# The relative-bias table of a two-layer decoder trunk: bucket runs copied on GpSimd in place of one-hot products on TensorE

## The chip, the cores and the metric

The kernel runs on one core of a Trainium2 chip. A core has TensorE (matrix products, written to PSUM), VectorE and ScalarE (which read PSUM and SBUF), GpSimd (SBUF only) and the queues that issue DMAs: SP's, ScalarE's and GpSimd's. In the profile they are called PE (with PEld for the loading of its weights), DVE, ACT, POOL and SP. Each engine works through its own instructions in order, and engines wait for each other through semaphores. The metric is the device time of one launch in microseconds (us), the median over the runs.

## The reference: what is computed

One sequence of 512 tokens with 1024 channels in float32 goes through two layers. Layer 0 is a Mamba-2 mixer and a convolutional feed-forward block. Layer 1 is differential attention (8 heads, two softmax maps for each) with shared keys and values, and a second feed-forward block. The part that matters here is the bias that is added to the attention logits:

```
n = max(dist, 0)                       # dist = query position - key position
bucket = n                 if n < 16
         16 + floor(log(n / 16) / log(8) * 16), at most 31   otherwise
bias[h] = rel_bias[bucket, h]          # rel_bias: 32 buckets x 8 heads
logits = q . k * scale + bias          # where dist < 0: -inf
```

The bias depends on the distance alone. A row of 512 distances for each head is therefore all that has to be known. Buckets 0 to 15 hold one distance each. From bucket 16 on, a bucket is a run of neighbouring distances, and the last one, 31, holds all distances from 113 up.

## The kernel before: how the work is ordered

All large products are made on TensorE from float32 values that are split in a high and a low part, so that one product is three passes (`mm3`, L196 to L198; in the attention's projections L932 to L934). The weights come in chunks of 512 KB on SP's queue (`wr_...`, three buffers). ScalarE makes the high part of each chunk (`wh_...`, L165 where a gain is folded in), VectorE the low part (`wl_...`, L166), and TensorE then reads both. Chunks are fetched two ahead of their use.

Between the feed-forward block of layer 0 and the attention of layer 1 lies the stage that the change touches. The order of TensorE's work there is written out by hand (`tc.manual_schedule` for PE) and the other engines are ordered by a planner:

- `ps_d`: the last products of the down-projection (L196 to L198). With them the sum of squares of the stream is collected in `nacc_kv` (L498, mostly on GpSimd).
- `ps_k` for the first half of the heads: `proj("k0")`, four token blocks in four PSUM banks, weights `wh_k`/`wl_k`. After the first chunk, `norm_kv.col()` turns `nacc_kv` (L445 on TensorE) and computes the factor of the RMS norm from it on VectorE in a chain of small steps (`tr_nkv`, L447 and L420 to L428). The evacuation of each `ps_k` bank multiplies by this factor (`knk`, ScalarE L954). Sums of squares (L955, L956), the norm of the heads (L434 to L439, L963) and transposes on TensorE (`ktk`, L970) follow.
- `ps_q` for the first half of the heads in the same four PSUM banks, with weights `wh_q`/`wl_q`.

The table is made at the start of this stage. `rb` holds `rel_bias` as it stands in memory (32 buckets on 32 partitions, 8 heads along the row). The array `onehot`, made on the host, has a row for each bucket and a column for each of 640 places (127 places for negative distances, then 513 for the distances from 0). Its two halves `oh` of 320 columns each are loaded, TensorE multiplies them by `rb` (`ps_rb`, L914), ScalarE copies the results to `bv` (L915), VectorE sets the negative distances to -1e30 (L917), and SP's queue writes both halves to a scratch table `bd` in memory (L918). For each head, a DMA on SP's queue (`tr`, L1000) reads the table shifted by one place on each of 128 partitions, and VectorE copies it in reversed order to `tb` (L1001), which the logits read at L1020. `tr` has one buffer, so the DMA of the next head waits for the copy of the one before.

SP's queue holds the weights of the following chunks and the DMAs of the table one behind the other; what is queued behind a DMA that waits, waits too.

Of the kernel before, what the change touches and what calls it, by code (L numbers as in the profile page):

```python
# [9 lines left out]
F32 = mybir.dt.float32  # L10
F32R = mybir.dt.float32r
I32 = mybir.dt.int32
AF = mybir.ActivationFunctionType
# [5 lines left out]
P = 128  # L19
# [12 lines left out]
AH = 8  # L32
EPS = 1e-6
NEG = -1.0e30
LAM_INIT = 0.8 - 0.6 * math.exp(-0.3 * 1)
NBIAS = 640
# [3 lines left out]
def trunk_kernel(ctx: ExitStack, tc, x, ssm_ln_g, ssm_in_w, ssm_conv_w, ssm_conv_b, ssm_dt_bias,  # L40
                 ssm_a_log, ssm_d, ssm_norm_g, ssm_out_w, kv_ln_g, kv_w, k_norm_g, rel_bias,
                 attn_ln_g, q_w, q_norm_g, lam_vecs, subln_g, attn_out_w, ffn_ln_g, ffn_up_w,
                 ffn_conv_w, ffn_conv_b, ffn_down_w, onehot, out):
    nc = tc.nc
    act, dve, pool, pe, sync = nc.scalar, nc.vector, nc.gpsimd, nc.tensor, nc.sync

# [13 lines left out]
    def aux_bank(name):  # L60
        return pp.tile([P, T], F32, tag="aux", name=name)
# [176 lines left out]
    with tc.tile_pool(name="ph0", bufs=1) as p0:  # L238
# [24 lines left out]
        ps = aux_bank("pst")  # L263
# [91 lines left out]
        for l in range(2):  # L355
            for j in range(2):
                cols = slice(j * FFN, (j + 1) * FFN)
                d = sf[:, 2 * l + j, :]
# [22 lines left out]
        ps = aux_bank("pst")  # L381
# [134 lines left out]
    with tc.tile_pool(name="ssm_y", bufs=1) as yp, tc.tile_pool(name="ssm", bufs=1) as sp:  # L516
# [29 lines left out]
        ps = aux_bank("ps_dtt")  # L546
# [32 lines left out]
        ps = aux_bank("ps_dec")  # L579
# [15 lines left out]
        ps = aux_bank("ps_cum")  # L595
# [304 lines left out]
    with tc.tile_pool(name="att_o", bufs=1) as op_, tc.tile_pool(name="att", bufs=1) as ap:  # L900
# [1 line left out]
        late = []  # L902


        rb = ap.tile([32, AH], F32, name="rb")
        bd = dp.tile([AH, NBIAS], F32, name="bd")
        sync.dma_start(rb, rel_bias)
        hb = NBIAS // 2
        for i in range(2):
            oh = ap.tile([32, hb], F32, tag="p0", name="oh%d" % i, bufs=3)  # L910
            bv = ap.tile([AH, hb], F32, tag="p1", name="bv%d" % i, bufs=3)
            sync.dma_start(oh, onehot[:, i * hb:(i + 1) * hb])
            ps = aux_bank("ps_rb%d" % i)
            pe.matmul(ps[:AH, :hb], rb, oh, start=True, stop=True)  # L914
            act.activation(bv, ps[:AH, :hb], AF.Copy)  # L915
            if i == 0:
                dve.memset(bv[:, 0:P - 1], NEG)  # L917
            sync.dma_start(bd[:, i * hb:(i + 1) * hb], bv)  # L918

        kT = [ap.tile([P, 4, T], F32, name="kT%d" % i) for i in range(2)]  # L920
        qT = [ap.tile([P, 4, T], F32, name="qT%d" % i) for i in range(2)]
# [249 lines left out]
    ffn(1, norm1, bp, None, None)  # L1171


def _onehot():
    dist = np.maximum(np.arange(NBIAS) - (P - 1), 0)
    nf = np.maximum(dist, 1).astype(np.float32)
    large = 16 + (np.log(nf / np.float32(16)) / np.float32(math.log(8)) * np.float32(16)).astype(np.int32)
    bucket = np.where(dist < 16, dist, np.minimum(large, 31))
    return np.ascontiguousarray((np.arange(32)[:, None] == bucket[None, :]).astype(np.float32))


_INS = ['x', 'ssm_ln_g', 'ssm_in_w', 'ssm_conv_w', 'ssm_conv_b', 'ssm_dt_bias', 'ssm_a_log', 'ssm_d',
# [25 lines left out]
```

## Time and profile before

| | before |
|---|---|
| time, median of 3 runs (lowest to highest) | 1356.53 us (1356.06 to 1356.53) |
| span of the profiled execution | 1355.4 us |
| median less span: what lies around the span | 1.1 us |
| TensorE busy | 1347.2 us (99%) |
| VectorE busy | 911.1 us (67%) |
| ScalarE busy | 654.0 us (48%) |
| GpSimd busy | 95.7 us (7%) |
| granted TensorE clock, mean | 0.999 |

The span runs from the first to the last instruction of one profiled execution. The busy time of an engine counts its compute instructions, not its waits. Rows of the timeline give the start, the duration, the engine, the line of the kernel, the operation, what it writes and reads and the shapes; in square brackets stands the time that the engine was idle before, and what ended this. SPq and POOLq are the queues that issue DMAs; their rows show the issue, not the transfer. Matrix products overlap, so their spacing from start to start is the better measure.

### The profile page before, as it was taken

To read this page: it belongs to the slowest core of one execution; us is meant where nothing else is said; L and a number is where in the kernel's file an instruction comes from. 1 tells how busy PE (TensorE), PEld (TensorE's weight loads), DVE (VectorE), ACT (ScalarE), POOL (GpSimd) and SP (SyncE) were. 2 spreads that over 40 slices of the span, in tenths; PEclk is the share of its full clock that TensorE was granted. 3 is DMA by queue.
4 is the path that set the end of the run, shared out by engine and by line. 5 is a ranking of instruction groups with operands and counts; after the bars stand their busy time and mean duration, and the time that the engine had idled before them with its cause. 6 is when DMAs were issued, how large, how long until landed. Compare 5 with 4: busy or idle time off the path is not lost.

```text
span 1355.4 us, 16857 instructions
## 1 busy us (share of the span) xinstructions
PE 1347.2 (99%) x6421; PEld 1096.1 (81%) x6421; DVE 911.1 (67%) x1525; ACT 654.0 (48%) x1066; POOL 95.7 (7%) x120
## 2 busy tenths in 40 slices
PE   9999999999999999999999999999999999999998
PEld 7877887887888888888888777777888888888887
DVE  4989878688777774267754555778777773367742
ACT  5696844642444442234433556767654442134420
POOL 6230301200020000000001000000110000000000
PEclk9999999999999999999999999999999999999999
DMA  7462432432333333333323422221223333333322
GB/s 203 138 170 78 149 109 94 148 94 69 95 94 93 94 96 105 94 94 94 101 78 108 127 80 86 78 75 37 78 87 89 104 94 94 93 104 99 94 94 78
DMA packets 179905, 135.06 MB, mean 100 GB/s; under 512 B 6509, under 2 KB 163633, under 8 KB 179825
## 3 DMA queue, kind: packets, MB, share of 16 engines
q1 hardware_dynamic: 174048, 120.84, 30.2%
q0 software_dynamic: 4496, 12.05, 2.9%
q8 instruction: 50, 0.82, 0.3%
q10 hardware_dynamic: 1280, 1.10, 0.2%
q14 instruction: 31, 0.25, 0.1%
HBM read 131.72 MB, written 2.25 MB: 99 GB/s over the span
## 4 chain that ended last, share of the span: by engine, by line
PE 94%; DVE 2%; ACT 1%; DMA 1%; issue 1%; POOL 0%; SPq 0%; DVEq 0%; POOLq 0%; ACTq 0%
PE ps_g L197 6%; PE ps_g L196 6%; PE ps_g L198 6%; PE ps_u L197 6%; PE ps_u L196 6%; PE ps_u L198 6%; PE ps_in L198 5%; PE ps_in L197 5%; PE ps_in L196 5%; PE ps_d L851 3%; PE ps_d L197 3%; PE ps_d L196 3%; PE ps_d L853 3%; PE ps_d L852 3%; PE ps_d L198 3%; PE ps_o L198 2%
## 5 line engine op out<-in xcount | busy, mean ns | idle before, releaser
L196 PE MATMUL ps_u<-xgh,wh_u 128*128 128x512 f32 x352 | 137.4, 390 | 0.0
L197 PE MATMUL ps_g<-xgl,wh_g 128*128 128x512 f32 x352 | 137.0, 389 | 0.0
L196 PE MATMUL ps_g<-xgh,wh_g 128*128 128x512 f32 x352 | 137.0, 389 | 0.0
L198 PE MATMUL ps_u<-xgh,wl_u 128*128 128x512 f32 x352 | 137.0, 389 | 0.0
L198 PE MATMUL ps_g<-xgh,wl_g 128*128 128x512 f32 x352 | 137.0, 389 | 0.0
L197 PE MATMUL ps_u<-xgl,wh_u 128*128 128x512 f32 x352 | 136.9, 389 | 0.0
L196 PE MATMUL ps_in<-xgh,wh_in 128*128 128x512 f32 x304 | 120.9, 398 | 0.0
L197 PE MATMUL ps_in<-xgl,wh_in 128*128 128x512 f32 x304 | 120.8, 397 | 0.0
L198 PE MATMUL ps_in<-xgh,wl_in 128*128 128x512 f32 x304 | 119.6, 393 | 0.0
L151 DVE TENSOR_TENSOR wl_d<-wr_d,wh_d 128x1024 fp32r<-128x1024 f32 (+1 forms) x46 | 54.2, 1178 | 96.9 <-ACT wh_d L147 96.7
L147 ACT ACTIVATE wh_d<-wr_d 128x1024 fp32r<-128x1024 f32 (+1 forms) x46 | 47.1, 1024 | 130.6 <-PE ps_d L853 62.4
L875 ACT ACTIVATE hh<-vg 128x512 fp32r<-128x512 f32 x44 | 27.8, 632 | 114.9 <-DVE vg L874 114.9
L823 DVE TENSOR_TENSOR uu<-ps_u,nr_f 128x512 f32<-128x512 f32 x44 | 30.4, 692 | 78.0 <-PE ps_u L198 77.8
L198 PEld LDWEIGHTS ps_g<-xgh,wl_g 128*128 128x128 f32 x352 | 66.1, 188 | 13.8
L197 PEld LDWEIGHTS ps_g<-xgl,wh_g 128*128 128x128 f32 x352 | 66.0, 187 | 13.9 <-DVE xgl L413 0.3
L197 PEld LDWEIGHTS ps_u<-xgl,wh_u 128*128 128x128 f32 x352 | 66.2, 188 | 13.5
L196 PEld LDWEIGHTS ps_g<-xgh,wh_g 128*128 128x128 f32 x352 | 66.1, 188 | 13.6
L196 PEld LDWEIGHTS ps_u<-xgh,wh_u 128*128 128x128 f32 x352 | 66.1, 188 | 13.7
L198 PEld LDWEIGHTS ps_u<-xgh,wl_u 128*128 128x128 f32 x352 | 66.0, 188 | 13.7
L147 ACT ACTIVATE wh_g<-wr_g 128x1024 fp32r<-128x1024 f32 x44 | 46.7, 1062 | 51.6 <-PE ps_u L197 32.2
L196 PE MATMUL ps_d<-hh,wh_d 128*128 128x512 f32 x176 | 68.5, 389 | 0.0
L197 PE MATMUL ps_d<-hl,wh_d 128*128 128x512 f32 x176 | 68.5, 389 | 0.0
(348 smaller groups left out, 3176.7 us busy)
## 6 DMA issues: line engine op xcount, KB each, us to landing
wr_g<-in_ffn_up_w_dram SPq DMA_DIRECT2D x44, 512.0 KB, 3.8
wr_u<-in_ffn_up_w_dram SPq DMA_DIRECT2D x44, 512.0 KB, 3.9
wr_d<-in_ffn_down_w_dram SPq DMA_DIRECT2D x42, 512.0 KB, 3.6
wr_in<-in_ssm_in_w_dram SPq DMA_DIRECT2D x40, 512.0 KB, 3.9
m<-cumd POOLq DMA_DIRECT2D x16, 512.0 KB, 4.0
wr_out<-in_ssm_out_w_dram SPq DMA_DIRECT2D x16, 512.0 KB, 3.5
wr_k<-in_kv_w_dram SPq DMA_DIRECT2D x8, 512.0 KB, 3.8
wr_q<-in_q_w_dram SPq DMA_DIRECT2D x8, 512.0 KB, 3.8
```

What stands on the lines that cost most here:

```text
L147: return act.activation(self.wh[:, :self.n], self.raw[:, :self.n], AF.Copy)
L151: return eng.tensor_tensor(out=self.wl[:, :self.n], in0=self.raw[:, :self.n], in1=self.wh[:, :self.n].bitcast(F32), op=ALU.subtract)
L196: pe.matmul(ps, wh, xh, start=start, stop=False)
L197: pe.matmul(ps, wh, xl, start=False, stop=False)
L198: return pe.matmul(ps, wl, xh, start=False, stop=stop).ins
L823: dve.tensor_tensor(out=u, in0=ps, in1=r, op=ALU.mult)
L851: pe.matmul(pss[b], hh[k][:, ts], wh[:, k - k0, :], start=k == 0, stop=False)
L852: pe.matmul(pss[b], hh[k][:, ts], wl[:, k - k0, :], start=False, stop=False)
L853: pe.matmul(pss[b], hl[k][:, ts], wh[:, k - k0, :], start=False, stop=k == n - 1)
L875: act.activation(h, ga, AF.Copy)
```

## The change

The one-hot array and both products go. `rb` becomes 8 partitions (heads) by 32 (buckets): a DMA on GpSimd's queue reads `rel_bias` transposed, each of the 256 values from its own place in memory. GpSimd then writes both halves `bv` itself: one memset for the 127 negative distances, one copy of 16 columns for the buckets 0 to 15, and one copy for each bucket from 16 to 31, in which a column of `rb` is repeated over the run. Bucket 31 crosses the middle at column 320 and takes two copies (80 and 320 columns). That makes 18 copies. The two halves go to `bd` by DMAs on GpSimd's queue too. From `tr` on, all is as before.

```diff
-        rb = ap.tile([32, AH], F32, name="rb")
+        rb = ap.tile([AH, 32], F32, name="rb")
         bd = dp.tile([AH, NBIAS], F32, name="bd")
-        sync.dma_start(rb, rel_bias)
+        pool.dma_start(rb, rel_bias.rearrange("b h -> h b"))
         hb = NBIAS // 2
         for i in range(2):
-            oh = ap.tile([32, hb], F32, tag="p0", name="oh%d" % i, bufs=3)
             bv = ap.tile([AH, hb], F32, tag="p1", name="bv%d" % i, bufs=3)
-            sync.dma_start(oh, onehot[:, i * hb:(i + 1) * hb])
-            ps = aux_bank("ps_rb%d" % i)
-            pe.matmul(ps[:AH, :hb], rb, oh, start=True, stop=True)
-            act.activation(bv, ps[:AH, :hb], AF.Copy)
             if i == 0:
-                dve.memset(bv[:, 0:P - 1], NEG)
-            sync.dma_start(bd[:, i * hb:(i + 1) * hb], bv)
+                pool.memset(bv[:, 0:P - 1], NEG)
+            for b, a, e in _ranges():
+                a, e = max(a - i * hb, 0), min(e - i * hb, hb)
+                if a < e:
+                    src = rb[:, 0:e - a] if b == 0 else rb[:, b:b + 1].to_broadcast([AH, e - a])
+                    pool.tensor_copy(bv[:, a:e], src)
+            pool.dma_start(bd[:, i * hb:(i + 1) * hb], bv)
...
+def _ranges():
+    dist = np.arange(NBIAS - (P - 1))
...
+    at = P - 1 + np.searchsorted(bucket, np.arange(33))
+    return [(0, P - 1, int(at[16]))] + [(b, int(at[b]), int(at[b + 1])) for b in range(16, 32)]
```

In the program that results, TensorE's order is the same but for the two products, and ScalarE's but for the two copies. On SP's queue the five DMAs of `rb`, `oh` and `bd` are gone. On GpSimd the DMA of `rb` and the memset stand ahead of the last addition to `nacc_kv` (L498), and the 18 copies and the two DMAs behind it. On VectorE the planner puts the first copy to `tb` (L1001) into the chain of `tr_nkv`: before, it stood behind the chain's last step; now it stands behind L423, with nine steps of the chain (three times L426, L427, L428) still to come.

More of the change, by code (lines that the diff above doesn't have):

```diff
@@ L42, in trunk_kernel @@
                  attn_ln_g, q_w, q_norm_g, lam_vecs, subln_g, attn_out_w, ffn_ln_g, ffn_up_w,
-                 ffn_conv_w, ffn_conv_b, ffn_down_w, onehot, out):
+                 ffn_conv_w, ffn_conv_b, ffn_down_w, out):
     nc = tc.nc
@@ L1171, in trunk_kernel @@
     ffn(1, norm1, bp, None, None)
-def _onehot():
-    dist = np.maximum(np.arange(NBIAS) - (P - 1), 0)
+def _ranges():
+    dist = np.arange(NBIAS - (P - 1))
     nf = np.maximum(dist, 1).astype(np.float32)
@@ L1178, in _onehot @@
     bucket = np.where(dist < 16, dist, np.minimum(large, 31))
-    return np.ascontiguousarray((np.arange(32)[:, None] == bucket[None, :]).astype(np.float32))
+    at = P - 1 + np.searchsorted(bucket, np.arange(33))
+    return [(0, P - 1, int(at[16]))] + [(b, int(at[b]), int(at[b + 1])) for b in range(16, 32)]
 _INS = ['x', 'ssm_ln_g', 'ssm_in_w', 'ssm_conv_w', 'ssm_conv_b', 'ssm_dt_bias', 'ssm_a_log', 'ssm_d',
@@ L1201 @@
         add("in_%s_dram" % name, np.ascontiguousarray(inputs[name]))
-    add("onehot_dram", _onehot())
     args.append(nc.dram_tensor("out_0_dram", (1, T, D), F32, kind="ExternalOutput").ap())
```

## The prediction

> **What bounds the kernel now.** I read first the page (busy time and the chain of waits), then the timeline of all engines around the removed products, then VectorE, SP's queue and GpSimd alone in that stage, last those who use what this stage makes. The page:
>
> ```profile
> span 1355.4 us, 16857 instructions
> ...
> PE 1347.2 (99%) x6421; PEld 1096.1 (81%) x6421; DVE 911.1 (67%) x1525; ACT 654.0 (48%) x1066; POOL 95.7 (7%) x120
> ...
> PE 94%; DVE 2%; ACT 1%; DMA 1%; issue 1%; POOL 0%; SPq 0%; DVEq 0%; POOLq 0%; ACTq 0%
> ```
>
> TensorE is busy nearly throughout and carries 94% of the chain. A stretch taken out of its stream shortens the time by its length, unless something else now makes TensorE wait; an edit elsewhere costs nothing until TensorE waits for it. GpSimd is nearly idle.
>
> **What goes from TensorE.** The timeline where the two products stand:
>
> ```profile
> 746.71 0.39 PE L933 MATMUL ps_k<-wl_k,xgh 128*128 128x512 f32 x1
> ...
> 747.17 0.39 PE L932 MATMUL ps_k<-wh_k,xgh 128*128 128x512 f32 x1
> ...
> 747.67 0.12 PEld L914 LDWEIGHTS ps_rb<-oh,rb 32*8 32x8 f32 x2 [0.54 <-PE ps_k L932]
> 747.71 1.23 PE L914 MATMUL ps_rb<-oh,rb 32*8 32x320 f32 x4
> 747.98 0.08 PEld L914 LDWEIGHTS ps_rb<-oh,rb 32*8 32x8 f32 x1 [0.18 <-DMA oh<-onehot_dram]
> ...
> 748.87 0.50 PE L933 MATMUL ps_k<-wl_k,xgh 128*128 128x512 f32 x1
> ...
> 749.20 0.39 PE L934 MATMUL ps_k<-wh_k,xgl 128*128 128x512 f32 x1
> ```
>
> Two steps of the stream take 747.17 - 746.71 = 0.46 us, so 0.23 each. From 747.17 to 749.20 there are again two steps, but 2.03 us: the products run as four instructions, with the change of weights around them and a short wait for `oh`. All of it goes: 2.03 - 0.46 = 1.57 us saved on the path. ScalarE's two copies, VectorE's memset and five DMAs of SP's queue go too; none stood in TensorE's way, so I count nothing for them.
>
> **What is added: when does the table arrive?** Call X the time, on the clock of this profile, at which VectorE can start the first copy to `tb`. SP's queue and VectorE before:
>
> ```profile
> 743.27 0.37 SPq L139 DMA_DIRECT2D wr_q<-in_q_w_dram  x1
> 744.00 0.35 SPq L907 DMA_DIRECT2D rb<-in_rel_bias_dram  x1
> ...
> 752.91 0.35 SPq L1000 DMA_DIRECT2D tr<-bd  x1
> 753.56 0.40 SPq L139 DMA_DIRECT2D wr_q<-in_q_w_dram  x1
> ```
> ```profile
> L918 SPq DMA_DIRECT2D bd<-bv x2: 271/342/412, 749.3 to 749.8; - x2
> ```
> ```profile
> 753.86 0.16 DVE L426 TENSOR_TENSOR rst_nkv<-tr_nkv 128x4 f32<-128x4 f32 x1
> ...
> 755.43 0.17 DVE L428 SCALAR_TENSOR_TENSOR tr_nkv<-rst_nkv,tr_nkv 128x4 f32<-128x4 f32 x1
> 756.29 0.43 DVE L1001 COPY tb<-tr 128x512 f32<-128x512 f32 x1 [0.69 <-DMA tr<-bd]
> 757.73 1.42 DVE L166 SCALAR_TENSOR_TENSOR wl_q<-wr_q,c,wh_q 128x512 fp32r<-128x512 f32 x2 [1.02 <-ACT wh_q L165]
> ...
> 772.53 2.50 DVE L963 TENSOR_TENSOR knk<-knk,ssk 128x512 f32<-128x512 f32 x4
> ```
>
> X was 756.29. GpSimd's rows, its small DMAs, and the only table in this kernel that GpSimd's queue writes to memory and reads back (`cumd`):
>
> ```profile
> 0.31 0.10 POOL L1193 MEMSET const-float32-0.0<- 128x1 f32 x1 [0.31 <-issue]
> 0.35 0.10 POOL L1193 MEMSET const-float32-1.0<- 128x1 f32 x1
> ...
> 1.15 0.29 POOL L204 TENSOR_SCALAR_AFFINE_SELECT ident<-ones 128x128 f32<-128x128 f32 x1 [0.63 <-DVE ones L202]
> ...
> 7.27 0.18 POOL L249 COPY xgo<-xt 128x1 f32<-128x1 f32 x1 [5.34 <-DMA xt<-in_x_dram]
> 7.40 0.71 POOL L250 DMA_DIRECT2D st<-in_ssm_conv_b_dram  x1
> ...
> 53.65 0.57 POOL L601 DMA_DIRECT2D cumd<-cumT  x1 [21.64 <-ACT c L236]
> ...
> 56.08 1.07 POOL L622 DMA_DIRECT2D m<-cumd  x2 [1.13 <-DMA cumd<-cumT]
> ```
> ```profile
> L632 POOL TENSOR_SCALAR_AFFINE_SELECT m<-m x16: 1085/1091/2010, 60.3 to 247.6; 128x1024 f32<-128x1024 f32 x16
> ```
> ```profile
> 745.65 1.42 POOL L498 TENSOR_TENSOR nacc_kv<-nacc_kv,nsq_kv 128x512 f32<-128x512 f32 x1 [10.55 <-ACT nsq_kv L496]
> ```
> ```profile
> cumd<-cumT POOLq DMA_DIRECT2D x2, 64.0 KB, 1.8
> ...
> alog<-in_ssm_a_log_dram POOLq DMA_DIRECT2D x1, 16.0 KB, 4.6
> ...
> s2t<-in_ssm_d_dram POOLq DMA_DIRECT2D x1, 0.1 KB, 5.5
> ...
> s2t<-in_subln_g_dram POOLq DMA_DIRECT2D x1, 0.5 KB, 2.9
> ```
>
> Step by step:
> - *Load of `rb`.* Before, SP was free at 743.64 and issued at 744.00, so the place of the tile comes free then. GpSimd, idle since before 745.65, issues at 744.0 too. It then has the memset and the issue (0.71 us at most in the rows) done by about 744.9, ahead of the addition to `nacc_kv` at 745.65, which is not delayed. Landing: 256 single values. The lower end is 2.9 us, one row of 0.5 KB. The nearest row is the one of the smallest pieces (`ssm_d`, 8 bytes each), 5.5 us, and I take that: 749.5. For the upper end, `alog` has 128 pieces and took 1.7 us more than the single row; twice the pieces make 3.4 us, and 6.8 us if eight rows spread over half as many DMA engines, which the trace doesn't show: 9.7 us.
> - *18 copies.* The nearest row is the copy of one column: 7.27 to 7.40, 0.13 us each, so 2.3 us; plus 400 long columns at (1.09 - 0.29) / 896 = 0.9 ns, 0.4 us. I take 2.7: 752.2. Ends: 0.04 us each (the two memsets' spacing), 1.1 us in all; 0.29 each (a select of 128 columns), 5.6 us.
> - *Two DMAs to `bd`.* The second is issued 0.6 us after the first (0.57 in `cumd`'s row). From issue to the reader's start `cumd` took 56.08 - 53.65 = 2.4 us, which I take: 755.2. Ends: 1.8 (landing alone) and 752.91 - 749.8 = 3.1 (SP's own pair before).
> - *`tr`.* 756.29 - 752.91 = 3.4 us, unchanged. X = 758.6; the lower ends give 753.8, the upper ones 766.4.
>
> **What waits behind it.** The planner moved the copy to `tb` into the middle of the chain of `tr_nkv`, so VectorE stands still before L426 until X. Behind it are nine small steps (753.86 to 755.60, 1.74 us), the low part of `wl_q` (1.42 us), and the next copy to `tb`. The factor r of the norm is ready at X + 0.43 + 1.74 = X + 2.2, that is 760.8 in place of 755.6. Those who need it:
>
> ```profile
> 763.72 0.69 ACT L954 ACTIVATE knk<-ps_k,tr_nkv 128x512 f32<-128x512 f32 x1
> ```
> ```profile
> 767.60 0.39 PE L932 MATMUL ps_q<-wh_q,xgh 128*128 128x512 f32 x1
> 767.83 0.39 PE L933 MATMUL ps_q<-wl_q,xgh 128*128 128x512 f32 x1
> ```
> ```profile
> 775.76 1.03 PE L970 MATMUL ktk<-ident,knk 128*128 128x128 f32 x8
> ...
> 796.94 1.23 PE L970 MATMUL ktq<-ident,knq 128*128 128x128 f32 x8 [0.16 <-DVE knq L963]
> ```
>
> TensorE's stream comes 1.57 us earlier, so the first evacuation would start at 762.15; r at 760.8 is in time. Had it been later, three things give way in turn. First the transposes: TensorE takes the first two blocks at 775.76, the second was ready at 772.53 + 1.25 = 773.78, so r may slip 2.0 us past 762.15, to 764.1, and X to 762.0. Then `wl_q` for the product at 767.83, now 766.26: ready at X + 3.6, so X up to 762.7. Then the bank of `ps_k`, needed at 767.60, now 766.03: r + 0.69, so X up to 763.2. On SP's queue the weights behind `tr` go out at X - 2.8 = 755.8, 2.2 us later than before, and are first used two chunks (48 steps, 11 us) after 766.0; the second head's row waits for the first copy as before and holds the next `wl_q`, needed one chunk after 766.0, with some 4 us in hand. So nothing reaches TensorE up to X = 762.0, 3.4 us above my value; beyond that each microsecond costs one. The sum: 1355.4 - 1.57 = 1353.8 us of span. The runs' median lies 1.1 us above the span, and that part is untouched: 1356.53 - 1.57 = 1355.0 us. This is -0.12%, under the 0.2% that a measurement can tell from no change here.
>
> One row speaks for slower copies: the same select took 1.09 us mostly and 2.01 once. Three such delays would add 2.8 us, X = 761.4, still covered. The Trainium skill (SBUF — State Buffer, Who interferes with whom) says that a GpSimd instruction that reads SBUF is shut out for the whole of a VectorE instruction with two SBUF inputs, if that came first. No row here shows which operation met the slow select; while the copies run only two or three such VectorE operations of some 0.75 us are left before VectorE itself stops for the table, so by that rule X is at most 760.9 and the sum the same, with a little more weight on the late case.
>
> **The rivals.**
> - *Late, but within the margin.* Several steps come near their upper ends, X between 762.0 and 766.2. With X = 764.3 (dearest copies and landing of `bd`, 758.6 + 2.9 + 0.7, and half of the 4.2 us that `rb` may take more), TensorE waits 2.3 us: 1355.0 + 2.3 = 1357.3. For it: the delay goes one to one through a chain of single waits. Against: no row asks for all at once.
> - *Slower: the transposed load.* One mechanism, the 256 single values of `rb`. The gain is spent when X reaches 762.0 + 1.57 = 763.5, a landing 10.4 us after the issue; slower by 0.2% from 13.1 us on. With twice the upper price of a piece it lands after 2.9 + 13.6 = 16.5 us, X = 769.6, TensorE waits 7.6 us: 1362.6. For it: no DMA of this kernel has so many pieces of 4 bytes. Against: the row of 8-byte pieces, 5.5 us. The Trainium skill (DMA: Bandwidth & Descriptors, Rules for kernel authors) warns of this very form: a strided last dimension becomes one descriptor per element. Its section on the anatomy of a DMA puts a small GpSimd DMA at about 2.0 us whatever it carries; an estimate by that figure has X at 755.1 and the time again at 1355.0. The rows here are all longer than that.
> - *The saved time is lost again further on,* 1356.5: some later wait of TensorE doesn't move with it. For it: the 0.16 us wait before `ktq`. Against: what it waits for begins with `ps_q`, TensorE's own work.
> - *More is saved than the stretch,* over 2.7 us: nothing in the profile shows where.
>
> **How the numbers follow.** Forecast 0.68 (own range 1354.4 to 1355.6, the spread of the runs); late 0.13; transposed load 0.11; lost again 0.05; more saved 0.03. Faster by over 0.2%: 0.03; within: 0.68 + 0.13 + 0.05 = 0.86; slower: 0.11. The range 1354.2 to 1358.5 takes in the late case nearly to its end and leaves out the last two tails.
>
> **What will show it.** Right: no row L914, steps of 0.23 us through 747 to 749, a GpSimd row of 18 copies ending near 752, VectorE idle before L1001 for some 5 us and TensorE without a new wait up to `ktk`. Wrong: a wait of TensorE on `knk`, `wl_q` or a bank of `ps_q`; `rb` landing after 754, copies over 0.3 us apart, or the DMA of `rb` issued later than 744 and pushing `nacc_kv` behind.

## The result, and the profile after

The changed kernel takes 1354.9 us (median of 21 runs, 1354.29 to 1355.5) where the kernel before takes 1356.53 (21 runs, 1355.72 to 1357.35). The ratio is 0.9987, with a 95% interval of 0.9981 to 0.9992. So the gain is some 1.6 us, on the side of "faster" but inside the 0.2% that I had called no change. I had forecast 1355.0.

The page of the kernel after, with its span, the busy times and the shares of the chain of waits:

```profile
span 1353.2 us, 16871 instructions
...
PE 1346.1 (99%) x6417; PEld 1096.0 (81%) x6417; DVE 911.4 (67%) x1524; ACT 654.0 (48%) x1064; POOL 102.6 (8%) x142
...
PE 94%; DVE 3%; ACT 1%; issue 1%; DMA 0%; POOL 0%; SPq 0%; DVEq 0%; ACTq 0%
```

TensorE has 4 instructions less and holds the end as before. The span is 2.2 us shorter, which is more than the products' stretch. To see what belongs to the change, take one stage only: from the first product of `ps_k` to the first transpose of `ktk`. TensorE works through it without a pause in both kernels, but for the short wait inside the products before, so its length depends on little else: in seven profiles without the products and without a wait of TensorE in it, it is 30.40 or 30.41 us, where the runs scatter by more than 1 us. In the timeline of TensorE, before:

```profile
743.77 0.39 PE L932 MATMUL ps_k<-wh_k,xgh 128*128 128x512 f32 x1
```

and after:

```profile
743.32 0.39 PE L932 MATMUL ps_k<-wh_k,xgh 128*128 128x512 f32 x1
...
747.17 0.39 PE L934 MATMUL ps_k<-wh_k,xgl 128*128 128x512 f32 x1
747.40 0.39 PE L932 MATMUL ps_k<-wh_k,xgh 128*128 128x512 f32 x1
...
773.73 1.03 PE L970 MATMUL ktk<-ident,knk 128*128 128x128 f32 x8
```

The stage lasted 775.76 - 743.77 = 31.99 us and lasts 773.73 - 743.32 = 30.41: 1.58 us less. No row of `ps_rb` is left and the steps are 0.23 us where the products stood. Of the other 0.6 us of the span 0.45 were there when the stage began, before anything of the change had run. That fits the scatter between executions: in the runs on record the span of the kernel before goes from 1354.4 to 1356.3. X, the start of the first copy to `tb`, is therefore counted from the start of the stage too: 756.29 - 743.77 = 12.5 before.

The table's way, in the timeline of the kernel after, GpSimd, VectorE and SP's queue:

```profile
743.78 0.74 POOL L907 DMA_DIRECT2D rb<-in_rel_bias_dram  x1 [9.12 <-PE ps_d L198]
744.52 0.20 POOL L912 MEMSET bv<- 8x127 f32 x1
745.22 1.41 POOL L498 TENSOR_TENSOR nacc_kv<-nacc_kv,nsq_kv 128x512 f32<-128x512 f32 x1 [0.50 <-ACT nsq_kv L496]
747.09 4.77 POOL L917 COPY bv<-rb 8x16 f32<-8x16 f32 x18 [0.46 <-DMA rb<-in_rel_bias_dram]
751.81 1.07 POOL L918 DMA_DIRECT2D bd<-bv  x2
754.25 0.34 SPq L1000 DMA_DIRECT2D tr<-bd  x1
757.87 0.43 DVE L1001 COPY tb<-tr 128x512 f32<-128x512 f32 x1 [5.78 <-DMA tr<-bd]
...
759.78 0.16 DVE L428 SCALAR_TENSOR_TENSOR tr_nkv<-rst_nkv,tr_nkv 128x4 f32<-128x4 f32 x1
```

The copies begin at 747.09, earlier than I had them, and end at 751.86, nearly where I had them (752.2), because they take 4.77 us in place of 2.7. X is 757.87 (14.55 from the start of the stage; forecast 14.83). VectorE stands still for 5.78 us, and TensorE doesn't notice.

### The profile page after: what moved, and what is told of

It is laid out like the page before. It is cut to its first block, busy times and chain, and to the rows that moved or that the text cites. A ratio compares the mean times of both kernels' runs of the same rounds, so it can differ in the third digit from the quotient of the medians.

```text
span 1353.2 us, 16871 instructions
## 1 busy us (share of the span) xinstructions
PE 1346.1 (99%) x6417; PEld 1096.0 (81%) x6417; DVE 911.4 (67%) x1524; ACT 654.0 (48%) x1064; POOL 102.6 (8%) x142
## 4 chain that ended last, share of the span: by engine, by line
PE 94%; DVE 3%; ACT 1%; issue 1%; DMA 0%; POOL 0%; SPq 0%; DVEq 0%; ACTq 0%
PE ps_g L197 6%; PE ps_g L196 6%; PE ps_g L198 6%; PE ps_u L196 6%; PE ps_u L197 6%; PE ps_u L198 6%; PE ps_in L197 5%; PE ps_in L196 5%; PE ps_in L198 5%; PE ps_d L851 3%; PE ps_d L196 3%; PE ps_d L852 3%; PE ps_d L197 3%; PE ps_d L853 3%; PE ps_d L198 3%; PE ps_o L198 2%
```

## The experiments

In this table the stage is the one above, and X is counted from its start. Each kernel is compared with runs of the kernel before on the same chip, whose median was 1356.5 to 1356.8.

| kernel | X | stage | median us | ratio to before, 95% |
|---|---|---|---|---|
| before | 12.5 | 31.99 | 1356.53 | |
| after | 14.55 | 30.41 | 1354.9 | 0.9987 (0.9981 to 0.9992) |
| products out, rest as before | | 30.40 | 1355.17 | 0.9990 (0.9981 to 0.9999) |
| after, two products back | | 31.79 | 1356.17 | 0.9994 (0.9985 to 1.0003) |
| 8 more copies | 16.54 | 30.40 | 1354.85 | 0.9987 (0.9978 to 0.9996) |
| 16 more copies | 18.89 | 32.25 | 1356.3 | 0.9997 (0.9989 to 1.0006) |
| 28 more copies | 21.57 | 35.29 | 1360.27 | 1.0025 (1.0015 to 1.0036) |
| 48 more copies | 27.21 | 39.75 | 1365.11 | 1.0058 (1.0046 to 1.0071) |
| 16 more, VectorE relieved | 18.32 | 30.40 | 1355.29 | 0.9988 (0.9979 to 0.9997) |
| 96 more, first copy to `tb` moved | 43.80 | 30.40 | 1366.07 | 1.0071 (1.0058 to 1.0083) |
| 40 more, two copies to `tb` moved | | 30.41 | 1354.98 | 0.9988 (0.9979 to 0.9997) |
| copies held until VectorE is still (one run) | 18.68 | 30.99 | 1355.8 | |
| `rb` in 8 rows (one run) | 14.39 | 30.40 | 1354.99 | |

### Is the gain TensorE's stretch and nothing else?

The two products alone are taken out of the kernel before:

```diff
-            ps = aux_bank("ps_rb%d" % i)
-            pe.matmul(ps[:AH, :hb], rb, oh, start=True, stop=True)
-            act.activation(bv, ps[:AH, :hb], AF.Copy)
+            act.activation(bv, oh[:AH], AF.Copy)
```

> The kernel before with nothing but the two one-hot products gone: all five DMAs on SP's queue, ScalarE's two copies and VectorE's memset stay (ScalarE copies eight rows of the one-hot array in place of the products' result, so the table holds no biases). Theory, the gain is TensorE's stretch alone: 1.57 us less than before, 1355.0, the same as the changed kernel. Rival, the gain lies with the other engines and queues that the change relieves: no difference to before, 1356.5. If each has a share, something between.

And two products of the same shape, from operands that are long there, are put back into the kernel after, with nobody reading them:

```diff
             pool.dma_start(bd[:, i * hb:(i + 1) * hb], bv)
+            ps = aux_bank("ps_rb%d" % i)
+            pe.matmul(ps[:AH, :hb], ident[:32, :AH], xTt[:32, KB - 1, :hb], start=True, stop=True)
```

> The changed kernel with two products of the same shape put back on TensorE, from operands that have long been there, result unread. Theory: the stretch returns without its short wait of 0.18 us for the one-hot rows, so 1.2 to 1.6 us more than the changed kernel, 1356.1 to 1356.5, and no gain over before. Rival, the gain lies with the other engines and queues: as the changed kernel, 1354.9.

Without the products (the table then holds no biases) the stage is 30.40 us long, as in the kernel after, with SP's queue, ScalarE's copies and the early table as they were. With them back it is 31.79. In the timeline of TensorE of that kernel one step of 0.23 has become 745.75 - 744.26 = 1.49 us:

```profile
744.26 0.39 PE L934 MATMUL ps_k<-wh_k,xgh 128*128 128x512 f32 x1
744.58 1.24 PE L920 MATMUL ps_rb<-xT,ident 32*8 32x320 f32 x4
745.75 0.50 PE L935 MATMUL ps_k<-wl_k,xgh 128*128 128x512 f32 x1
```

So the gain is the place in TensorE's stream. Products from ready operands cost 31.79 - 30.41 = 1.38 of the 1.58 us; the other 0.2 are about the 0.18 us of wait for `oh` in the row shown of before.

### How late may the table be?

The second half's DMA is put off by copies that write the same 14 columns again, and the first copy to `tb` is held where it is, between L423 and L426 of the chain (`first_copy` holds the DMA to `tr` and the copy of head 0, unchanged):

```diff
+            for _ in range(N * i):
+                pool.tensor_copy(bv[:, 0:14], rb[:, 31:32].to_broadcast([AH, 14]))
             pool.dma_start(bd[:, i * hb:(i + 1) * hb], bv)
...
+        if name == "nkv":
+            pin(two)
+            pin(first_copy())
```

with N = 48 first:

> The changed kernel with 48 further copies of 14 columns on GpSimd ahead of the second write of the table, which makes the table late; VectorE's first copy of the table is held at its place in the chain of the norm's factor. At 0.125 us a copy (the spacing of the undisturbed ones in the changed kernel) the table comes 6.0 us later, X = 763.9. Theory, free until X = 761.5 on that kernel's clock, then one to one: 2.4 us more than the changed kernel, 1357.3, with TensorE waiting at the first transposes of k. Rival, lateness counts from the first microsecond: 6 us more, 1360.9. Rival, other work covers it all: 1354.9.

The added copies took 0.265 us each, about twice what I had. Unlike the 18, they all write the same columns from the same one; that each waits for the one before is my reading, not shown. So X went to 27.21, further than planned, and the planner put a pair of `wl_q` ahead of the copy. The loss in the stage is 39.75 - 30.41 = 9.34 us, of which some 1.4 are slow steps of TensorE after its wait (last section). The rival that other work covers it all falls; where a slack ends, this run can't say. With the price of a copy known, three smaller N followed:

> The changed kernel with 8 further copies of 14 columns on GpSimd ahead of the second DMA to bd (they write the same columns again, 0.25 us each by the 48 measured); the first copy to tb held in its place between L423 and L426. X comes 2.0 us later, 757.87 + 2.0 = 759.9. Theory of a slack, with the place taken from the changed kernel's profile: the factor may be ready up to 763.66, so X up to 761.5; nothing reaches TensorE: 1354.9. Rival, lateness counts from the first microsecond because VectorE's later work moves with it: 1356.9.

> The same with 16 copies: X 4.0 us later, 761.9, just past the end of the slack: theory 0.4 us, 1355.3. Rival, no slack: 1358.9.

> The same with 28 copies, of which one or two run at 0.7 us: X 7 to 7.6 us later, about 765.3. The planner puts half of wl_q into the chain behind the copy to tb, so the factor is ready about 768.2, 4.5 us past 763.66. Theory, one to one beyond the slack: 1359.5. Rival, no slack: 1362.5. Rival, VectorE's later idle time takes it up: 1354.9.

With 8 copies the stage is 30.40: 2.0 us more lateness cost nothing, which is the slack itself. With 16 the loss is 32.25 - 30.41 = 1.84 us in the stage and 1.4 in the median. The theory had 0.4 (0.7 at the X that came) and the rival 4.0, so the slack is there but ends sooner than I read it: at X = 18.89 - 1.84 = 17.05, if it is one to one from there, and for this order of VectorE's work in any case between 16.54 and 18.89. My limit was 762.0 - 743.77 = 18.2. The rows of the kernel with 16 copies show why (here L931 and L1017 are the two copies to `tb`, L970 the sums of squares, L977 the normalisation, L968 and L969 ScalarE's evacuation and squares, L946 and L984 TensorE's products and transposes). Timeline, all engines:

```profile
761.90 0.43 DVE L931 COPY tb<-tr 128x512 f32<-128x512 f32 x1 [10.12 <-DMA tr<-bd]
...
763.91 1.41 DVE L166 SCALAR_TENSOR_TENSOR wl_q<-wr_q,c,wh_q 128x512 fp32r<-128x512 f32 x2
764.80 0.63 ACT L969 ACTIVATE ksqk<-knk 128x512 f32<-128x512 f32 x1
...
765.35 0.43 DVE L1017 COPY tb<-tr 128x512 f32<-128x512 f32 x1
765.69 1.41 DVE L166 SCALAR_TENSOR_TENSOR wl_q<-wr_q,c,wh_q 128x512 fp32r<-128x512 f32 x2
767.01 0.68 DVE L970 TENSOR_REDUCE ssk<-ksqk 128x8 f32<-128x512 f32 x1
...
767.79 0.63 ACT L969 ACTIVATE ksqk<-knk 128x512 f32<-128x512 f32 x1 [1.78 <-DVE ssk L970]
768.33 0.67 ACT L968 ACTIVATE knk<-ps_k,tr_nkv 128x512 f32<-128x512 f32 x1
...
769.05 0.50 PE L946 MATMUL ps_q<-wh_q,xgh 128*128 128x512 f32 x1 [0.93 <-ACT knk L968]
...
775.26 1.17 PE L984 MATMUL ktk<-ident,knk 128*128 128x128 f32 x8 [0.38 <-DVE knk L977]
```

The first square was ready by 765.43, but its sum starts at 767.01: VectorE first does `wl_q`, the second head's `tb` and `wl_q` again, 3.3 us that stand behind the factor in its queue. ScalarE has one buffer for the squares and waits for the sum (1.78 us), so the third bank of `ps_k` is emptied late and TensorE waits for it (0.93), and then for the normalised blocks (0.38). I had followed the factor into ScalarE, and not the queue behind it on VectorE.

With 28 copies the loss in the stage is 4.88 us and in the median 5.4, at X = 21.57: by the corrected end it would be 4.5. There the planner had put half of the first pair of `wl_q` ahead of the copy and half into the chain, so the end need not be the same. "One to one beyond the slack" holds roughly: from 16 to 48 copies X grows by 8.3 us and the stage by 7.5. "VectorE's idle time takes it up" falls.

### Is it VectorE's queue that ends the slack?

The kernel with 16 copies again, with two edits that take work from VectorE behind the factor: ScalarE, idle there, writes the second pair of `wl_q` (the scaled weights, without the subtraction that makes them the low part), and the second head's copy to `tb` stands behind the normalisation of `q0`.

```diff
+                if self.key == "q0_2":
+                    act.activation(wl[:, ks], self.raw[:, ks], AF.Copy, scale=g)
+                    continue
...
+                        with tc.issue_after(state["q0"].ins):
+                            dve.tensor_copy(st["tb"], tr[:, ::-1])
```

> The kernel with 16 further copies, with VectorE's work between the factor and the first sum of squares cut down: the low part of the second pair of wl_q is not computed (ScalarE, idle there, writes the scaled weights in its place, so the output isn't the reference's), and the second head's copy to tb stands behind the normalisation of q0. X stays near 761.9. Theory, it is VectorE's queue behind the factor (wl_q, tb, wl_q, 3.3 us) that shortened the slack: the first sum starts near 765.5 in place of 767.01, TensorE has no wait inside ps_q, and before ktk 0.4 to 0.8 us; 1355.5. Rival, the factor alone sets the end, by a limit 1.4 us earlier than I read: waits as with 16 copies before, 1356.3.

The timeline of VectorE of that kernel (L934 is the first copy to `tb`, L973 the sums, L980 the normalisation):

```profile
761.32 0.43 DVE L934 COPY tb<-tr 128x512 f32<-128x512 f32 x1 [9.55 <-DMA tr<-bd]
...
765.30 0.69 DVE L973 TENSOR_REDUCE ssk<-ksqk 128x8 f32<-128x512 f32 x1 [0.57 <-ACT ksqk L972]
...
772.07 2.50 DVE L980 TENSOR_TENSOR knk<-knk,ssk 128x512 f32<-128x512 f32 x4
```

The first sum waits for ScalarE now, not for VectorE's own work, and starts 4.0 us after X in place of 5.1. TensorE has no wait, neither in `ps_q` nor before `ktk`, where I had still expected 0.4 to 0.8 us: the stage is 30.40, all of the 1.84 us is back. X came 0.57 us earlier from the stage's start than with 16 copies, so the lateness alone could have given back that much, not the rest. VectorE's queue is shown as what ended the slack.

A kernel from further below ("Why did the 18 copies take 4.77 us?"), whose 18 copies are held until VectorE is still, points the same way without that edit. The timeline of VectorE (L932 is the first copy to `tb`, L971 the sums):

```profile
755.96 1.42 DVE L166 SCALAR_TENSOR_TENSOR wl_q<-wr_q,c,wh_q 128x512 fp32r<-128x512 f32 x2 [3.90 <-ACT wh_q L165]
762.29 0.43 DVE L932 COPY tb<-tr 128x512 f32<-128x512 f32 x1 [4.92 <-DMA tr<-bd]
...
766.35 0.68 DVE L971 TENSOR_REDUCE ssk<-ksqk 128x8 f32<-128x512 f32 x1
```

Its X is 18.68, only 0.21 us less than with 16 copies, but the planner put the first pair of `wl_q` ahead of the wait. The first sum starts 4.1 us after X, and the stage loses 30.99 - 30.41 = 0.58 us in place of 1.84. One to one from there, the slack ends at 18.1, about my limit: it held for a factor with less work of VectorE behind it. So there is no one end of the slack; it goes by the order in VectorE's queue.

### Does the lateness cost anything outside that chain?

Here the table comes late, but the copies to `tb` of the first two heads stand behind the normalisations of `k0` and `q0` instead of in the chain of `tr_nkv`:

```diff
-                    dve.tensor_copy(st["tb"], tr[:, ::-1])
+                    if h > 1:
+                        dve.tensor_copy(st["tb"], tr[:, ::-1])
+                    else:
+                        with tc.issue_after(state["q0" if h else "k0"].ins):
+                            dve.tensor_copy(st["tb"], tr[:, ::-1])
```

A first form of it, with 96 copies and only head 0 moved so:

> The changed kernel with 96 further copies on GpSimd (12 us at 0.125 us each, X = 769.9 if VectorE were to wait there), but with VectorE's first copy of the table put behind the norm of the first k block, some 14 us further on. Theory, lateness costs only through what VectorE has queued behind the copy: as the changed kernel, 1354.9 within 0.4. Rival, the late table also costs through SP's queue, where weights stand behind the reading of the table, or through the logits: 1356 to 1363. The further copies now run beside a working VectorE, so they should be further apart on average than the 0.125 us of those that run while VectorE stands still, if its instructions are what stretched some of the 18 copies to 0.7 us.

What was expected was missed by 11 us (median 1366.07), and the run doesn't decide the question: 96 copies took 28.7 us, the table came at 787.63, after the new place too, and VectorE waited for it there, 12.77 us. The stage itself was 30.40; TensorE waited in the next one. With 40 copies:

> The changed kernel with 40 further copies (10 to 12 us), and the first copy to tb put behind the normalisation of k0 (near 774 on VectorE), that of the second head behind that of q0. The table comes near 769, before the copy's new place. Theory, the table's lateness costs only through the place that the copy has in the chain of tr_nkv: 1354.9, within 0.4. Rival, it costs by itself, through the DMA of the second head's row, held on SP's queue with the weights behind it: 1356 to 1366.

The timeline of GpSimd and VectorE with 40 copies:

```profile
752.33 11.67 POOL L919 COPY bv<-rb 8x14 f32<-8x14 f32 x40
764.29 0.52 POOL L920 DMA_DIRECT2D bd<-bv  x1 [0.29 <-POOL bv L919]
...
774.20 0.42 DVE L1007 COPY tb<-tr 128x512 f32<-128x512 f32 x1
```

The second half left GpSimd 11.9 us later than in the kernel after, the copy to `tb` had no wait, and stage (30.41) and median (1354.98) are as after. SP's queue, whose later weights stand behind `tr`, cost nothing. In these kernels the lateness costs through one thing: the place of a copy in VectorE's queue.

### Why did the 18 copies take 4.77 us?

Single copies in the kernel after, from short stretches of its timeline, beside what VectorE does at that time:

```profile
747.09 0.75 POOL L917 COPY bv<-rb 8x16 f32<-8x16 f32 x1 [0.46 <-DMA rb<-in_rel_bias_dram]
747.10 0.68 DVE L498 TENSOR_TENSOR nacc_kv<-nacc_kv,nsq_kv 128x512 f32<-128x512 f32 x1
747.71 0.74 DVE L166 SCALAR_TENSOR_TENSOR wl_k<-wr_k,c,wh_k 128x512 fp32r<-128x512 f32 x1
747.79 0.70 POOL L917 COPY bv<-rb 8x3 f32<-8x3 f32 x1
...
750.75 0.80 DVE L166 SCALAR_TENSOR_TENSOR wl_k<-wr_k,c,wh_k 128x512 fp32r<-128x512 f32 x1
750.95 0.91 POOL L917 COPY bv<-rb 8x320 f32<-8x320 f32 x1
751.47 0.41 DVE L421 TENSOR_SCALAR tr_nkv<-rsm_nkv 128x4 int32<-128x4 int32 x1
```

Each slow copy lies beside an operation of VectorE with two inputs from SBUF. To tell this from the copies' own shapes, the 18 were held until VectorE has finished the step ahead of its wait (`fill` holds the loop of the copies):

```diff
+            pin(two)
+            fill(v)
+            pin(first_copy())
...
+                if i == 0:
+                    pin(pool.tensor_copy(bv[:, 0:4], v[:AH]))
+                    pool.memset(bv[:, 0:P - 1], NEG)
```

> The changed kernel with GpSimd's 18 copies held until VectorE has finished the step ahead of its wait for the table (one copy of 4 columns from that step's result in front of them). Theory, the three copies of 0.7 us and the slow one of 320 columns met VectorE's operations with two SBUF inputs: alone they take 2.6 us, 0.125 apart, none over 0.3 but the last at 0.4 to 0.5. Rival, these shapes or places are slow by themselves: 4.7 us again, with the same copies at 0.7. Time near 1355 in either case.

The timeline of VectorE and GpSimd then:

```profile
751.69 0.17 DVE L421 TENSOR_SCALAR tr_nkv<-rsm_nkv 128x4 int32<-128x4 int32 x1
...
752.12 0.18 POOL L919 COPY bv<-tr_nkv 8x4 f32<-8x4 f32 x1 [5.21 <-DVE tr_nkv L423]
...
752.51 2.26 POOL L925 COPY bv<-rb 8x16 f32<-8x16 f32 x17
755.06 0.55 POOL L926 DMA_DIRECT2D bd<-bv  x1 [0.29 <-POOL bv L925]
755.60 0.44 POOL L925 COPY bv<-rb 8x320 f32<-8x320 f32 x1
```

Alone the copies take 2.26 + 0.44 = 2.70 us, what I had summed, and the one of 320 columns 0.44 in place of 0.91. So 2.1 us of the 4.77 came from VectorE, whose four operations with two inputs met the copies. In the kernel with the two products put back only two of the four did, and the copies took 3.61 us. It looks like exclusive use and not like a slower pace: a copy of 3 columns lasts as long as VectorE's operation beside it. VectorE pays too: its L421 took 0.41 us beside the long copy, and 0.17 here, with GpSimd still. The Trainium skill (SBUF — State Buffer, Who interferes with whom) says that an operation of VectorE with two SBUF inputs and a GpSimd instruction that reads SBUF need the same port, and that whoever comes first has it for the whole instruction. The rows of the copies agree. L421 reads one tensor only, so this sentence doesn't cover its delay, and no run here shows which such operations are held.

### Are 256 single values dear to load?

```diff
-        pool.dma_start(rb, rel_bias.rearrange("b h -> h b"))
+        pool.dma_start(rb, rel_bias.rearrange("(a c) h -> a (c h)", a=AH))
```

> The changed kernel with rb loaded as 8 rows of 32 neighbouring values (128 bytes each) in place of 256 single values; the table then holds other biases, so the output isn't the reference's. Theory, a small load costs its fixed part whatever the pieces: landing 2.9 to 3.3 us beside 3.2 of the single values. Rival, the single values cost time that the queue's other work hides: 2 us or less.

The view of the DMA issues of this kernel (its last number is the time from issue to landing in us):

```profile
rb<-in_rel_bias_dram POOLq DMA_DIRECT2D x1, 1.0 KB, 3.3
```

and of the kernel after:

```profile
rb<-in_rel_bias_dram POOLq DMA_DIRECT2D x1, 1.0 KB, 3.2
bd<-bv POOLq DMA_DIRECT2D x2, 10.0 KB, 1.7
```

8 pieces of 128 bytes land no sooner than 256 of 4 bytes, which took 3.2 to 3.6 us over the profiles of all kernels that load so. At this size the form of the load costs nothing that shows in the landing.

## Why the prediction was right, point by point

The forecast of 1355.0 met 1354.9. It rests on one term that was right, and on a margin in which several sizes were off and partly cancelled.

- *What goes from TensorE.* Right: 1.57 forecast, 1.58 in the stage, and both kernels that move the products alone confirm it. The copies of ScalarE, the memset and the five DMAs on SP, which I had put at nothing, cost nothing: with them the stage is 30.40, without them 30.41.
- *Median and span.* The 1.1 us that I put around the span is no such thing: in every run on record the time lies 1.65 to 1.97 us above the run's own span (1354.9 and 1353.2 for the kernel after). The profiled execution of before was some 0.6 us longer than the usual one. The forecast of the median doesn't use the term; the span forecast of 1353.8 was too high by these 0.6 us.
- *Load of `rb`.* The issue was right (743.78; the addition to `nacc_kv` at 745.22 is not delayed). The landing was mis-sized: 5.5 us forecast, 3.2 measured. I had chosen the row with the smallest pieces; at this size the piece count has no share that shows. The row of one 0.5 KB piece, 2.9, was the near one. The rival of the dear transposed load falls with it. The rule of the Trainium skill (DMA: Bandwidth & Descriptors, Rules for kernel authors) that I had set beside it, one descriptor per element, to be avoided, is no cost at 1 KB. The fixed 2.0 us of the same page of the Trainium skill (Anatomy of one DMA) would have been too little by 1.2.
- *18 copies.* The price of an undisturbed copy was right (2.70 us in all). The step that failed is the one that set VectorE aside: I allowed the contention up to 2.3 us in X and didn't count it, and it took 2.1. The trace of before had a sign of it: the slow select that I had quoted, 2.01 us in place of 1.09, starts at 62.28, beside VectorE's L657 with two inputs from SBUF (62.06 to 63.34), and 1.09 us after that is about its end.
- *DMAs to `bd` and `tr`.* 754.25 - 751.81 = 2.4 us from the first issue to `tr`'s, where I had 3.0; then 757.87 - 754.25 = 3.6, where I had 3.4. The first is at the lower end of its bounds; the second had none and is 0.2 longer.
- *X and r.* 14.55 us from the start of the stage against 14.83. The errors of 2.3 us in the landing and 2.1 in the copies cancelled; that the sum came out near is luck. The second alone would have put X at 16.9, at the edge of the slack. The factor is ready 2.07 us after X (2.2 forecast).
- *The slack.* The step that failed is "First the transposes": that the factor could slip by all of the 2.0 us. I took the time from the factor to the normalised blocks from a stage paced by ScalarE and let the whole of it move. When the factor is late, VectorE's 3.3 us behind it (of which I had named the first `wl_q` and the next copy to `tb`) come ahead of the first sum, and the banks and the blocks are late sooner. With VectorE's order as in the changed kernel the end is near 17.05 (if one to one from there), not 18.2, so the margin was some 2.5 us and not the 3.4 that I gave it; with my X it would have been 2.2. The late case was nearer than its chance of 0.13 rests on, though not by enough to come true.
- *Beyond the slack one to one.* Right in the rough, from 16 to 48 copies: 7.5 us of stage for 8.3 of X, with the order on VectorE not the same and a share of slow steps in the last. *SP's queue and the later weights*: right, no wait.
- *Lost again, or more saved.* Neither. The wait of 0.16 us before `ktq` is there as before.

What stays open is the gain in the runs to better than about 0.7 us: the interval reaches from 0.8 to 1.9 thousandths. The stage says 1.58 us.

## What to carry to other kernels

Moving a small piece of work off the engine that holds the end gained its stretch in that engine's stream here, no more; whether it stays gained depends on who stands still for the later result, and on all that stands behind that one in its queue, also after the result is in. Measure a change of a thousandth by the length of the stage it touches in one profile, not by the runs alone. When small GpSimd operations are to run beside VectorE, count the VectorE operations with two SBUF inputs that will meet them: here four cost 2.1 us.

## What the runs showed of the hardware that I had not expected

GpSimd's small copies start some 0.13 us apart when they write different columns (2.26 us for 17). When all write the same columns, they start 0.24 apart with VectorE still, in the kernel with 16 copies:

```profile
752.03 3.88 POOL L924 COPY bv<-rb 8x14 f32<-8x14 f32 x16
```

With VectorE at work beside them it was 0.29 (11.67 us for 40, shown above).

After a wait TensorE may first run at half its pace. The timeline of TensorE in the kernel with 28 copies:

```profile
767.98 0.72 PE L946 MATMUL ps_q<-wh_q,xgh 128*128 128x512 f32 x1 [2.62 <-ACT knk L968]
768.50 0.63 PE L947 MATMUL ps_q<-wl_q,xgh 128*128 128x512 f32 x1
...
771.06 0.60 PE L947 MATMUL ps_q<-wl_q,xgh 128*128 128x512 f32 x1
771.48 0.41 PE L948 MATMUL ps_q<-wh_q,xgl 128*128 128x512 f32 x1
```

And two stretches of the same kernel, with the busy time and the count of instructions of TensorE, its weight loads, VectorE, ScalarE and GpSimd, then the granted clock of TensorE, the share of the DMA engines and their GB/s:

```profile
768.00:771.50 3.50, 3.50 (x9) 2.76 (x10) 2.40 (x5) 1.88 (x4) 0.00 (x0) 0.51 0.64 209
771.50:776.00 4.50, 4.50 (x21) 3.71 (x20) 3.24 (x5) 3.45 (x6) 0.00 (x0) 1.00 0.38 109
```

The steps are 0.43 us (771.06 to 771.48) for 3.5 us, at a granted clock of 0.51, and then 0.23 again. With 28 copies TensorE had to wait for `knk` once more before `ktk` (0.21 us), so the slow steps were covered. With 48 copies the wait was 7.72 us and no second one followed: the slow steps, about 1.4 us, are part of the loss of 9.34. After the wait of 0.93 us with 16 copies the steps were 0.23 to 0.24. The Trainium skill (TensorE: Matmul & The Clock Gate, What's actually happening) gives about 3.4 us of idleness for the fall to half the clock and as much busy time for the return. The return agrees (3.5 us here); the fall came here after a wait of 2.62 us.
